# Second block's attention in a one-core network kernel: TensorE's order written out by hand, scores and transposes of a head in one stretch each

## The chip, the core and the metric

The kernel runs on one core of one Trainium2 chip. The metric is device time in microseconds (us) from start to end of one execution, as the median of several runs; lower is better. Engines are named as in the profile: PE is TensorE's matmul, PEld its weight load, DVE is VectorE, ACT is ScalarE, SP issues the DMAs.

## What is computed

The reference chains two transformer blocks on 512 tokens of width 1024. The change concerns the attention at the start of the second one, the "even" mixer: 8 heads of windowed attention (two key/value heads, distances up to 128, a slope on the distance and a learned sink) and 8 heads of neighbourhood attention (8 by 16 neighbours, learned bias), all with a root-mean-square norm per head on queries and keys:

```python
def _even_mixer(x, norm_g, w_in, qn_a, kn_a, sink_a, qn_b, kn_b, rpb_b, w_out):
    h = _rmsnorm(x, norm_g)
    qa, ka, va, qb, kb, vb = _split(h @ w_in, EVEN_SPLITS)
    qa = _rmsnorm(qa.reshape(B, S, A_KV_HEADS, A_GROUP, HEAD_DIM), qn_a)
    ka = _rmsnorm(ka.reshape(B, S, A_KV_HEADS, HEAD_DIM), kn_a)
    oa = _window_gqa(qa, ka, va, sink_a)
    qb = _rmsnorm(qb.reshape(B, S, B_HEADS, HEAD_DIM), qn_b)
    kb = _rmsnorm(kb.reshape(B, S, B_HEADS, HEAD_DIM), kn_b)
    ob = _neighbourhood_attn(qb, kb, vb, rpb_b)
    return jnp.concatenate([oa, ob], axis=-1) @ w_out
```

Its result is added to the residual `x`; a wide MLP (`mlp(0)`) follows.

## The kernel before

Everything is kept feature by token: a tile is 128 features by 512 tokens. Every fp32 product is made of three fp32r products of a high and a low half (`mm3`, L272 to L274), so every operand is first split: ACT casts the high half (`split` L286, `weight` L315) and DVE subtracts to get the low half (L287, L316). Eight PSUM banks are handed out by tag (`ps`): acc 3, sc 2, pt 2, o 1.

The stage `even` runs four kinds of step, each a generator:

- g (`begin`): one projection of 24 products of 512 columns into an acc bank, scaled by DVE (L1311), squared by ACT (L1313). f (`finish`): for a query or key tile, the column total on PE into a pt bank (L419, `total`), then the reciprocal root (`rsqrt`, ACT L295, L296, DVE L297 to L299), the gain (L1317) and the split; for a value tile, four transposes into a pt bank (L1338).
- A, B (`window`) and C, D (`neighbours`): four heads each, three steps a head, all in `softmax`. Scores: four query blocks of 128, with 256, 384, 384 and 256 keys, each in its own sc bank, three products each; DVE adds the bias and takes the maximum (L488), ACT exponentiates (L495). Then DVE multiplies by the reciprocal sum (L502), PE transposes ten 128 by 128 pieces into four pt banks (L510) and each bank is split into `Ph` and `Pl`. Then the product with the values, twelve products into the o bank, copied out by ACT (L520, or L1343 for the neighbourhood heads) to `y`.
- o (`result`): splits of the finished `y` tiles and first parts of the output projection `w_out_e`.

`EVEN_ORDER` (L69) is the order in which the program asks for these steps. It sets priorities only: a scheduler then places every instruction on its engine by its own estimate, so on PE products of projections, scores, transposes and values are mixed one by one. Each engine then runs its list strictly in order.

After the last head, `rest` finishes the output projection; `residual` (L593) adds it to `X`, and `mlp` prepares its operands from `X` two tiles at a time (`seven_x` L1472 to L1474 and splits, `seven_w` L1486 to L1488 for the weights) for the first group of MLP products (`seven_mm`).

Of the kernel before, what the change touches and what calls it, by code (L numbers as in the profile page):

```python
# [25 lines left out]
T = 512  # L26
D = 1024
# [38 lines left out]
CROSS_ORDER = "q00q01211023312233"  # L66


EVEN_ORDER = "gggfgggffgAfBgffAgfCABCDgBgADBCDAgffffBCDfBgCggADBAfgfDAfDfCCgBACfDABCBgABfCDADoBCoDCoDo"  # L69

ODD_ORDER = (
    "apggpgppapagagpaaappgpagapapaapaaapaapgapagapaaapaagappgaapaaagpagapagagpagaapaoaaagpaggpagaappa"
# [166 lines left out]
class Kernel:  # L239
# [232 lines left out]
    def softmax(self, q, k, V, e, qblk, kblk, bias, sink, y, evac):  # L472

        nc = self.nc
        qo, ko = _offsets(qblk), _offsets(kblk)
        pr = slice(64 * e, 64 * e + 64)
        P = self.tl(self.pa, [128, 1280], F32, "P", self.n_p)  # L480
        st = self.tl(self.pt, [128, 20], F32, "st", 6)
        mx, nm, sm, rs, es = (st[:, 4 * i:4 * i + 4] for i in range(5))
        for i, (c0, w) in enumerate(qblk):
            ps = self.ps("sc")
            qs = slice(128 * i, 128 * i + 128)
            self.mm3(ps[:, :w], (q[0][pr, qs], q[1][pr, qs]),
                     (k[0][pr, c0:c0 + w], k[1][pr, c0:c0 + w]), True, True)
            nc.vector.tensor_tensor_reduce(P[:, qo[i]:qo[i] + w], ps[:, :w], bias(i), 1.0,  # L488
                                           -3e38 if sink is None else sink, ALU.add, ALU.max, mx[:, i:i + 1])
        nc.vector.tensor_scalar(nm, mx, -1.0, None, op0=ALU.mult)  # L490
        if sink is not None:
            nc.scalar.activation(es, nm, AF.Exp, bias=sink)
        for i, (c0, w) in enumerate(qblk):
            b = P[:, qo[i]:qo[i] + w]
            nc.scalar.activation(b, b, AF.Exp, bias=nm[:, i:i + 1], accum_out=sm[:, i:i + 1])  # L495
        yield
        if sink is not None:
            nc.vector.tensor_tensor(sm, sm, es, op=ALU.add)
        nc.vector.reciprocal(rs, sm)
        for i, (c0, w) in enumerate(qblk):  # L500
            b = P[:, qo[i]:qo[i] + w]
            nc.vector.tensor_scalar(b, b, rs[:, i:i + 1], None, op0=ALU.mult)  # L502
        Ph = self.tl(self.pa, [128, 1280], F32R, "Ph", 2)
        Pl = self.tl(self.pa, [128, 1280], F32R, "Pl", 2)
        for j, (t0, w) in enumerate(kblk):
            pt = self.ps("pt")
            for c in range(0, w, 128):
                i = (t0 + c) // 128
                at = qo[i] + 128 * j - qblk[i][0]
                nc.tensor.transpose(pt[:, c:c + 128], P[:, at:at + 128], self.ident)  # L510
            sl = slice(ko[j], ko[j] + w)
            self.split(Ph[:, sl], Pl[:, sl], pt[:, :w])
        yield
        o = self.ps("o")
        first = True
        for j, (t0, w) in sorted(enumerate(kblk), key=lambda z: -z[1][1]):
            sl = slice(ko[j], ko[j] + w)
            self.mm3(o[:64, t0:t0 + w], V(j), (Ph[:, sl], Pl[:, sl]), first, True)
            first = False
        evac(y[pr], o[:64])  # L520
        yield

# [767 lines left out]
    def even(self):  # L1290
        nc, A = self.nc, self.A
        with self.tc.tile_pool(name="even", bufs=1) as pa:
# [1 line left out]
            xs, r, first = self.nxt()  # L1294
            rel = pa.tile([128, 384], F32, name="rel")
            nc.scalar.dma_start(rel, A["c_rel"])
            gq = pa.tile([128, 2], F32, name="gq")
            for i, n in enumerate(("q_norm_a_2", "q_norm_b_2")):
                nc.vector.tensor_scalar(gq[:, i:i + 1], self.vec(n), 0.125, None, op0=ALU.mult)
            ys = [self.tl(pa, [128, T], F32, "y", 8) for _ in range(8)]  # L1300
            self.n_p = 3

# [4 lines left out]
            def qk(name, m, gain, perm=False):  # L1307
# [4 lines left out]
                q = self.s()  # L1312
                nc.scalar.activation(q, t, AF.Square)  # L1313
                yield
                rs = self.s()
                self.rsqrt(rs, self.total(q, mat=self.hsum), 64, RMS_EPS, tmp=q)
                nc.vector.scalar_tensor_tensor(q, t, gain, rs, op0=ALU.mult, op1=ALU.mult)  # L1317
                h, l = (self.tl(pa, [128, T], F32R, "qk", 10) for _ in range(2))
                if perm:
# [26 lines left out]

            jobs, env = [], {}
            put = lambda key, gen, *args: jobs.append((key, gen(*args)))
            put("k", qk, "w_e_a", 0, self.vec("k_norm_a_2"))
            put("v", value, "w_e_a", 1)  # L1350
            put(("q", 0), qk, "w_e_a", 2, gq[:, 0:1])
            put(("q", 1), qk, "w_e_a", 3, gq[:, 0:1])
            for a in range(4):
                put(("nq", a), qk, "w_e_b", 3 * a, gq[:, 1:2], True)
                put(("nk", a), qk, "w_e_b", 3 * a + 1, self.vec("k_norm_b_2"), True)
                put(("nv", a), value, "w_e_b", 3 * a + 2, True)
                if a < 2:
                    put(("q", a + 2), qk, "w_e_a", a + 4, gq[:, 0:1])

            def begin():  # L1360
                for _, gen in jobs:
# [9 lines left out]
            def window(e):  # L1371
                for a in range(4):
                    b = self.tl(pa, [128, 384], F32, "gb", 2)
                    with self.tc.issue_after(env["normed"]):
                        nc.vector.tensor_scalar(b, rel, -(2.0 ** -(a + 4 * e + 1)), None, op0=ALU.mult)
                    bias = lambda i: b[:, 128 * (i == 0):128 * (i == 0) + BAND_Q[i][1]]
                    yield from self.softmax(env["q", a], env["k"], self.vat(env["v"], e), e, BAND_Q, BAND_K, bias,
                                            self.vec("sink_a_2", a + 4 * e), ys[a], nc.scalar.copy)

            def neighbours(e):  # L1380
                for a in range(4):
                    b = self.tl(pa, [128, 896], F32, "nb", 2)
                    nc.sync.dma_start(b, A["na_bias"][2 * a + e])
                    bias = lambda i: b[:, (0, 256, 256, 640)[i]:(0, 256, 256, 640)[i] + BAND_Q[i][1]]
                    yield from self.softmax(env["nq", a], env["nk", a], self.vat(env["nv", a], e), e, BAND_Q, BAND_K,
                                            bias, None, ys[4 + a], unperm)

            yh, yl = [None] * NK, [None] * NK
            begun = []
            early = [0, 4, 1, 5, 2, 6]  # L1390

            def split_y(ks):
                for k in ks:
                    yh[k], yl[k] = self.xtile(), self.xtile()
                    self.split(yh[k], yl[k], ys[k])

            def out(m, w, ps, ks, start, stop):
                for k in ks:
                    self.mm3(ps, (w[0][k], w[1][k]), (yh[k], yl[k]), start and k == ks[0], stop and k == ks[-1])

            def result():
                split_y(early)
                yield
                for m in range(3):
                    begun.append((self.weight("w_out_e", m, 128), self.ps()))
                    out(m, *begun[m], early, True, False)
                    yield

            run = {"g": begin(), "f": finish(), "A": window(0), "B": window(1), "C": neighbours(0),
                   "D": neighbours(1), "o": result()}  # L1410
            for c in EVEN_ORDER:
                next(run[c])
            for gen in run.values():
                assert next(gen, None) is None
            split_y([3, 7])

            def rest(m):
                if m < 3:
                    out(m, *begun[m], [3, 7], False, True)
                    return begun[m][1]  # L1420
                return self.gemm("w_out_e", m, (yh, yl))

# [330 lines left out]
```

## Time and profile before

| what | value |
|---|---|
| median of 3 runs | 2172.0 us (2170.09 to 2173.36) |
| profiled execution | 2170.15 us |
| its span, first to last instruction | 2168.4 us |
| busy share of the span: PE, DVE, ACT | 98%, 72%, 53% |
| chain that ended last: PE, DVE, ACT | 89%, 6%, 2% |
| first PE instruction that the change moves | 824.8 us |
| last value product of the attention | 1013.5 us |
| first product of the MLP's first group | 1039.2 us |

A PE row's duration contains pipeline time, so neighbouring products overlap in the table; what a product occupies is the distance from its start to the next start. "PE busy" therefore stays near 100% even where starts lie far apart. In a window's row the numbers are us of busy time, in brackets the count of instructions.

### The profile page before, as it was taken

What the parts mean: (1) busy time and instruction counts of PE and PEld (TensorE: products, weight loads), DVE (VectorE), ACT (ScalarE), POOL (GpSimd) and SP (SyncE); (2) the same over time, 40 slices, a digit from 0 to 9 for tenths busy, and PEclk for the clock granted to TensorE, in tenths of its full rate; (3) what the DMA queues carried; (4) which work ended last, traced back from release to release, by engine and by line L of the source; (5) the groups of instructions that cost most, each with busy time, mean ns of one, the idle gap of its engine ahead of it and who ended that gap; (6) DMA issues with size and microseconds to landing.
All of it is one profiled execution on the core that took longest, in us unless ns stands there. A gap on an engine that the chain in (4) does not pass through costs nothing.

```text
span 2168.4 us, 31653 instructions
## 1 busy us (share of the span) xinstructions
PE 2134.2 (98%) x11942; PEld 1804.8 (83%) x11942; DVE 1564.8 (72%) x2863; ACT 1150.8 (53%) x2100; POOL 6.0 (0%) x22
## 2 busy tenths in 40 slices
PE   8999999899999999999999999999999999999999
PEld 7877788788888897777889889888888888898997
DVE  8867858787774268887978576756776579875864
ACT  6555656665553256667645344555555456453542
POOL 0000000000000000000000000000000000000000
PEclk9999999999999999999999999999999999999999
DMA  5211241133233322211333231322222233322321
GB/s 174 70 64 64 78 142 59 49 102 102 93 98 90 91 79 85 75 65 54 128 106 101 94 106 51 112 81 78 69 71 86 68 107 117 108 98 98 106 70 68
DMA packets 94760, 192.66 MB, mean 89 GB/s; under 512 B 10512, under 2 KB 12176, under 8 KB 94608
## 3 DMA queue, kind: packets, MB, share of 16 engines
q1 hardware_dynamic: 93744, 189.01, 26.8%
q8 instruction: 93, 1.52, 0.3%
q10 hardware_dynamic: 864, 1.64, 0.2%
q14 instruction: 59, 0.48, 0.1%
HBM read 188.52 MB, written 2.10 MB: 88 GB/s over the span
## 4 chain that ended last, share of the span: by engine, by line
PE 89%; DVE 6%; ACT 2%; DMA 1%; issue 1%; SPq 0%; DVEq 0%; ACTq 0%
PE acc L272 20%; PE acc L273 20%; PE acc L274 19%; PE sc L272 6%; PE sc L274 5%; PE sc L273 5%; PE pt L274 2%; PE pt L272 2%; PE pt L273 2%; PE o L272 2%; PE o L273 2%; PE o L274 2%; PE pt L510 1%; PE sc L903 1%; PE pt L419 1%; DVE wl L316 1%
## 5 line engine op out<-in xcount | busy, mean ns | idle before, releaser
L315 ACT CAST wh<-wf 128x512 fp32r<-128x512 f32 (+1 forms) x548 | 333.9, 616 | 532.9 <-PE acc L273 429.8
L316 DVE TENSOR_TENSOR wl<-wf,wh 128x512 fp32r<-128x512 f32 (+1 forms) x548 | 369.2, 682 | 181.2 <-ACT wh L315 168.1
L272 PE MATMUL acc<-x,wh 128*128 128x512 f32 (+1 forms) x1104 | 425.2, 388 | 6.4 <-ACT x L280 5.4
L273 PE MATMUL acc<-x,wh 128*128 128x512 f32 (+1 forms) x1104 | 423.9, 385 | 0.2
L274 PE MATMUL acc<-x,wl 128*128 128x512 f32 (+1 forms) x1104 | 423.8, 385 | 0.0
L272 PEld LDWEIGHTS acc<-x,wh 128*128 128x128 f32 x1104 | 207.8, 189 | 53.0 <-ACT x L280 6.2
L273 PEld LDWEIGHTS acc<-x,wh 128*128 128x128 f32 x1104 | 208.2, 189 | 44.8 <-issue 2.9
L274 PEld LDWEIGHTS acc<-x,wl 128*128 128x128 f32 x1104 | 208.1, 189 | 43.8 <-issue 2.2
L286 ACT CAST Wh<-F 128x1792 fp32r<-128x1792 f32 x64 | 108.2, 1693 | 100.4 <-PE pt L273 66.9
L287 DVE TENSOR_TENSOR Wl<-F,Wh 128x1792 fp32r<-128x1792 f32 x64 | 129.2, 2020 | 30.9 <-ACT Wh L286 30.2
L274 PE MATMUL acc<-y,wl 128*128 128x512 f32 x288 | 113.7, 395 | 0.0
L273 PE MATMUL acc<-y,wh 128*128 128x512 f32 x288 | 113.6, 395 | 0.0
L272 PE MATMUL acc<-y,wh 128*128 128x512 f32 x288 | 113.3, 393 | 0.0
L272 PE MATMUL acc<-wh,x 128*128 128x256 f32 (+1 forms) x352 | 98.9, 281 | 0.3 <-DVE v L281 0.3
L274 PE MATMUL acc<-wh,x 128*128 128x256 f32 (+1 forms) x352 | 98.8, 281 | 0.0
L273 PE MATMUL acc<-wl,x 128*128 128x256 f32 (+1 forms) x352 | 98.8, 281 | 0.0
L274 PE MATMUL sc<-x,wl 128*128 128x512 f32 (+1 forms) x264 | 96.2, 366 | 1.1 <-DVE wl L316 1.1
L273 PE MATMUL sc<-x,wh 128*128 128x512 f32 (+1 forms) x264 | 96.0, 366 | 0.9 <-DVE x L281 0.7
L272 PE MATMUL sc<-x,wh 128*128 128x512 f32 (+1 forms) x264 | 95.0, 366 | 1.5 <-ACT x L280 1.2
L272 PE MATMUL acc<-h,wh 128*128 128x512 f32 (+1 forms) x220 | 74.1, 337 | 0.0
L274 PE MATMUL acc<-h,wl 128*128 128x512 f32 (+1 forms) x220 | 74.1, 337 | 0.0
L273 PE MATMUL acc<-h,wh 128*128 128x512 f32 (+1 forms) x220 | 74.1, 337 | 0.0
(510 smaller groups left out, 5119.9 us busy)
## 6 DMA issues: line engine op xcount, KB each, us to landing
F<-in_w_mlp_in_dram SPq DMA_DIRECT2D x64, 512.0 KB, 3.2
wf<-in_w_mlp_out_dram SPq DMA_DIRECT2D x128, 256.0 KB, 2.8
wf<-in_w_ffn_in_dram SPq DMA_DIRECT2D x88, 256.0 KB, 2.7
wf<-in_w_o_fm_dram SPq DMA_DIRECT2D x64, 256.0 KB, 2.7
wf<-in_w_in_fm_dram SPq DMA_DIRECT2D x44, 256.0 KB, 2.8
wf<-in_w_ffn_out_dram SPq DMA_DIRECT2D x40, 256.0 KB, 2.7
wf<-in_w_o_v_dram SPq DMA_DIRECT2D x32, 256.0 KB, 3.1
wf<-in_w_out_o_dram SPq DMA_DIRECT2D x32, 256.0 KB, 2.8
```

Of the source, the lines that this page charges most:

```text
L272: mm(ps, lhsT=lh, rhs=rh, start=start, stop=False, skip_group_check=True)
L273: mm(ps, lhsT=lh, rhs=rl, start=False, stop=False, skip_group_check=True)
L274: self.last_mm = mm(ps, lhsT=ll, rhs=rh, start=False, stop=stop, skip_group_check=True).ins
L286: nc.scalar.copy(hi, src)
L287: nc.vector.tensor_tensor(lo, src, self.f(hi), op=ALU.subtract)
L315: nc.scalar.copy(h[:, :n], wf[:, :n])
L316: nc.vector.tensor_tensor(l[:, :n], wf[:, :n], self.f(h[:, :n]), op=ALU.subtract)
L419: self.last_total = self.nc.tensor.matmul(ps[:, :n], lhsT=self.ones if mat is None else mat, rhs=acc[:, :n], start=True, stop=True).ins
L510: nc.tensor.transpose(pt[:, c:c + 128], P[:, at:at + 128], self.ident)
L903: mm = lambda out, pr, ss, ts: nc.tensor.matmul(out, lhsT=kq[0][pr, ss], rhs=kq[1][pr, ts], start=True, stop=True, skip_group_check=True)
```

## The change

Only `even` changes. `band_head` replaces `softmax` for these 16 heads: scores go to three banks (two blocks of 256 keys share one; the third bank is an acc bank for the first twelve heads, an sc bank for the last four), the ten transposes to three banks (the third is acc, then pt). Two of the four normalisations of a head move from DVE to ACT (`AF.Identity`, L568 of after). In `qk` one of the three DVE steps of the reciprocal root becomes an ACT square. The output projection is begun for five of its eight tiles before the end of the attention, in place of three. And the loop over `EVEN_ORDER` stands in a `manual_schedule` for PE: there the instructions keep the program's order. The letters now are g, f, o as before and S (scores of the next head), T (its transposes), V (its value product); heads follow `EVEN_HEADS`.

```diff
-EVEN_ORDER = "gggfgggffgAfBgffAgfCABCDgBgADBCDAgffffBCDfBgCggADBAfgfDAfDfCCgBACfDABCBgABfCDADoBCoDCoDo"
+EVEN_ORDER = (
+    "gggggg" "fff" "g" "f" "S" "TSgV" "TffSgV" "TfSgV" "TfSgV" "TfSgV" "TfSgV" "TfSgV" "TfSgV" "TfSgV" "TfSgV"
+    "TffSgV" "TfSoV" "TfSoV" "TSoV" "TSVo" "ToVo")
+EVEN_HEADS = "ABABCDABCDABCDCD"
...
+    def band_head(self, q, k, V, e, bias, sink, y, evac, third):
...
+        at = (0, 512, 896, 256)
+        banks = ((0, 3), (1,), (2,))
+        order = (0, 3, 1, 2)
...
+        for tag, tiles in zip(("sc", "sc", third[0]), banks):
+            ps, c, got = self.ps(tag), 0, []
+            for i in tiles:
+                k0, w = BAND_Q[i]
+                qs = slice(128 * i, 128 * i + 128)
+                self.mm3(ps[:, c:c + w], (q[0][pr, qs], q[1][pr, qs]), (k[0][pr, k0:k0 + w], k[1][pr, k0:k0 + w]),
+                         c == 0, True)
+                got.append((i, ps[:, c:c + w]))
+                c += w
+            for i, p in got:
+                red = nc.vector.tensor_tensor_reduce(part(i), p, bias(i), 1.0, -3e38 if sink is None else sink,
+                                                     ALU.add, ALU.max, mx[:, i:i + 1])
...
+        for i in order:
+            nc.scalar.activation(part(i), part(i), AF.Exp, bias=nm[:, i:i + 1], accum_out=sm[:, i:i + 1])
+        yield
...
+        for i in order:
+            if i in banks[0]:
+                nc.vector.tensor_scalar(part(i), part(i), rs[:, i:i + 1], None, op0=ALU.mult)
+            else:
+                nc.scalar.activation(part(i), part(i), AF.Identity, scale=rs[:, i:i + 1])
...
+        for tag, tiles in zip(("pt", "pt", third[1]), banks):
+            pt, c = self.ps(tag), 0
+            for j in tiles:
+                t0, w = BAND_K[j]
+                for i in range(t0 // 128, (t0 + w) // 128):
+                    b = at[i] + 128 * j - BAND_Q[i][0]
+                    nc.tensor.transpose(pt[:, c:c + 128], P[:, b:b + 128], self.ident)
+                    c += 128
+            sl = slice(at[tiles[0]], at[tiles[0]] + c)
+            self.split(Ph[:, sl], Pl[:, sl], pt[:, :c])
+        yield
...
-                rs = self.s()
-                self.rsqrt(rs, self.total(q, mat=self.hsum), 64, RMS_EPS, tmp=q)
+                rs, v = self.s(), self.total(q, mat=self.hsum)
+                nc.scalar.activation(rs, v, AF.Ln, scale=1.0 / 64, bias=self.eps_col[:, 0:1])
+                nc.scalar.activation(rs, rs, AF.Exp, scale=-0.5)
+                nc.scalar.activation(q, rs, AF.Square, scale=math.sqrt(0.5 / 64))
+                nc.vector.scalar_tensor_tensor(q, v, 64 * RMS_EPS, q, op0=ALU.add, op1=ALU.mult)
+                nc.vector.scalar_tensor_tensor(rs, q, -1.5, rs, op0=ALU.add, op1=ALU.mult)
...
             def result():
-                split_y(early)
-                yield
-                for m in range(3):
-                    begun.append((self.weight("w_out_e", m, 128), self.ps()))
-                    out(m, *begun[m], early, True, False)
+                first = [0, 4, 1, 5, 2]
+                split_y(first)
+                for m, tag in enumerate(("acc", "acc", "acc", "sc", "sc")):
+                    begun.append((self.weight("w_out_e", m, 128), self.ps(tag)))
+                    if m == 1:
+                        split_y([3])
+                        out(0, [3])
+                    if m < 4:
+                        out(m, first + [3] * (m > 0), True)
+                    else:
+                        out(m, first[:4], True)
                     yield
+                out(4, [2, 3])
+                yield
...
+            third = lambda: ("acc", "acc") if len(started) < 12 else ("sc", "pt")
...
-            for c in EVEN_ORDER:
-                next(run[c])
+            with self.tc.manual_schedule(engines={mybir.EngineType.PE}):
+                for c in EVEN_ORDER:
+                    next(run[c])
```

How the change moves instructions shows at three places. In the lists the names are those of the tiles (cm holds the identity and the matrix of the totals), and the last field is the size.

First place: PE, from the scores of the first head (the sc and first acc tiles) to its transposes (P is the head's row of probabilities). Before, the last scores and what follows them:

```order
L274 MATMUL acc_8399<-x_7765,wl_8390 128x512
L272 MATMUL acc_8399<-x_7767,wh_8389 128x512
L272 MATMUL sc_8328<-qk_8163,qk_8269 128x384
L273 MATMUL sc_8328<-qk_8164,qk_8269 128x384
L274 MATMUL sc_8328<-qk_8163,qk_8270 128x384
L272 MATMUL sc_8333<-qk_8163,qk_8269 128x256
L273 MATMUL sc_8333<-qk_8164,qk_8269 128x256
L274 MATMUL sc_8333<-qk_8163,qk_8270 128x256
L273 MATMUL acc_8399<-x_7768,wh_8389 128x512
```

After:

```order
L277 MATMUL acc_8349<-qk_8253,qk_8273 128x384
L278 MATMUL acc_8349<-qk_8254,qk_8273 128x384
L279 MATMUL acc_8349<-qk_8253,qk_8274 128x384
L577 MATMUL pt_8368<-cm,P_8333 128x128 x4
L577 MATMUL pt_8375<-cm,P_8333 128x128 x3
L577 MATMUL acc_8381<-cm,P_8333 128x128 x3
L277 MATMUL sc_8391<-qk_8253,qk_8273 128x256
```

Before, 55 rows (projections, the second head's scores, two totals) stand between this head's last scores and its first transposes; after, none.

Second place: PE at the turn from the first head's values to the second head's transposes; Ph, Pl and v are the operands of the value product, s the squared query tile of a total, 'waits' names the engine whose signal is awaited. Before, at such a turn further on:

```order
L274 MATMUL o_8561<-Ph_8460,v_1569_8148 64x256
L510 MATMUL pt_8583<-cm,P_8359 128x128 x2
L510 MATMUL pt_8588<-cm,P_8359 128x128 x3
L272 MATMUL sc_8638<-qk_8450,qk_8437 128x256
L273 MATMUL sc_8638<-qk_8451,qk_8437 128x256
L274 MATMUL sc_8638<-qk_8450,qk_8438 128x256
```

After:

```order
L279 MATMUL o_8457<-Ph_8366,v_1569_8152 64x384
L577 MATMUL pt_8479<-cm,P_8389 128x128 [waits DVE_49,PE_49]
L577 MATMUL pt_8479<-cm,P_8389 128x128 [waits Activation_49] x2
L577 MATMUL pt_8479<-cm,P_8389 128x128 [waits DVE_49]
L577 MATMUL pt_8486<-cm,P_8389 128x128 [waits PE_49]
L577 MATMUL pt_8486<-cm,P_8389 128x128 x2
L577 MATMUL acc_8492<-cm,P_8389 128x128 [waits PE_49]
L577 MATMUL acc_8492<-cm,P_8389 128x128 x2
L424 MATMUL pt_8499<-s_8201,cm 128x512 [waits DVE_49]
L424 MATMUL pt_8512<-s_8242,cm 128x512 [waits DVE_49]
L277 MATMUL sc_8528<-qk_8253,qk_8327 128x256
```

After, the totals of f, which need a pt bank, stand right behind the transposes that have just filled both.

Third place: ACT at the same turn, where the copy of the first head's values stands ahead of the casts that empty the second head's banks. After:

```order
L587 COPY y_8138<-o_8457 64x512
L291 CAST Ph_8477<-pt_8479 128x512
L291 CAST Ph_8477<-pt_8486 128x384
L291 CAST Ph_8477<-acc_8492 128x384
L1385 ACTIVATE s_8498<-pt_8499,eps 128x512
```

Before, such a turn reads so, with banks of 256 and 384 columns:

```order
L520 COPY y_8136<-o_8704 64x512
L315 CAST wh_9180<-wf_9178 128x512
L315 CAST wh_9186<-wf_9184 128x512
L286 CAST Ph_8794<-pt_8796 128x256
L286 CAST Ph_8794<-pt_8801 128x384
```

The copy and the casts are the same work; after, the first bank holds 512 columns.

## Rows read from the trace of the kernel before

**Rows 1.** The page, part 1: busy us (share of the span), instructions

```profile
PE 2134.2 (98%) x11942; PEld 1804.8 (83%) x11942; DVE 1564.8 (72%) x2863; ACT 1150.8 (53%) x2100; POOL 6.0 (0%) x22
```

**Rows 2.** Windows: stretch, length, busy us (count) of each engine, granted clock, DMA

```profile
950.00:960.00 10.00, 9.75 (x46) 6.48 (x44) 8.38 (x23) 6.56 (x14) 0.00 (x0) 1.00 0.34 111
...
1020.00:1030.00 10.00, 10.00 (x45) 8.08 (x44) 10.00 (x19) 8.77 (x15) 0.00 (x0) 1.00 0.62 210
```

**Rows 3.** Waits of PE, 800 to 1060 us: total us, times, longest

```profile
PE acc L272 <- ACT x L280: 1.4, 1, 1.4
PE sc L272 <- ACT qk L286: 0.6, 2, 0.4
```

**Rows 4.** Timeline of PE: start, us, line, tiles, shapes, count; projections, values, scores

```profile
650.64 0.39 PE L273 MATMUL acc<-x,wh 128*128 128x512 f32 x1
650.87 0.39 PE L274 MATMUL acc<-x,wl 128*128 128x512 f32 x1
...
864.38 0.28 PE L274 MATMUL o<-Ph,v 128*64 128x256 f32 x1
864.59 0.44 PE L272 MATMUL sc<-qk,qk 64*128 64x384 f32 x1
864.87 0.33 PE L273 MATMUL sc<-qk,qk 64*128 64x384 f32 x1
865.04 0.33 PE L274 MATMUL sc<-qk,qk 64*128 64x384 f32 x1
...
867.51 0.34 PE L274 MATMUL sc<-qk,qk 64*128 64x384 f32 x1
867.78 0.50 PE L274 MATMUL acc<-x,wl 128*128 128x512 f32 x1
868.12 0.39 PE L272 MATMUL acc<-x,wh 128*128 128x512 f32 x1
```

**Rows 5.** Chain that ended last, 820 to 1060 us: start, us, what

```profile
866.24 0.55 PE pt L510 x5
...
941.33 2.19 ACT P L495 x8
```

**Rows 6.** Timeline of all engines: the last value products and what follows them

```profile
1011.81 0.34 PE L272 MATMUL o<-Ph,v 128*64 128x384 f32 x1
...
1013.54 0.28 PE L274 MATMUL o<-Ph,v 128*64 128x256 f32 x1
...
1013.86 1.07 ACT L1343 COPY y<-o 64x512 f32<-64x512 f32 x1 [1.68 <-PE o L274]
```

**Rows 7.** Timeline: split of a PSUM bank of 512 columns

```profile
1001.94 0.59 ACT L286 CAST v<-pt 128x512 fp32r<-128x512 f32 x1 [1.29 <-PE pt L1338]
...
1002.56 0.69 DVE L287 TENSOR_TENSOR v<-pt,v 128x512 fp32r<-128x512 f32 x1 [0.36 <-ACT v L286]
```

**Rows 8.** Groups by line and form, 800 to 1060 us: busy us, mean ns, idle before

```profile
L502 DVE TENSOR_SCALAR P<-P,st 128x256 f32<-128x256 f32 x32 | 10.9, 344 | 0.1
...
L488 DVE CUSTOM_DVE_ANT_0 P<-sc,gb,vecs 128x384 f32<-128x384 f32 x16 | 9.8, 613 | 1.3 <-PE sc L274 1.2
...
L297 DVE SCALAR_TENSOR_TENSOR s<-s 128x512 f32<-128x512 f32 x13 | 8.8, 687 | 3.0 <-ACT s L296 2.9
...
L1343 ACT COPY y<-o 64x512 f32<-64x512 f32 x8 | 8.7, 1084 | 3.2 <-PE o L274 3.1
...
L488 DVE CUSTOM_DVE_ANT_0 P<-sc,gb,vecs 128x256 f32<-128x256 f32 x16 | 7.6, 476 | 2.1 <-PE sc L274 2.1
...
L520 ACT COPY y<-o 64x512 f32<-64x512 f32 x8 | 4.6, 575 | 3.3 <-PE o L274 3.2
```

**Rows 9.** Timeline of DVE and PE at the end of the MLP's first group

```profile
1051.08 2.49 DVE L316 TENSOR_TENSOR wl<-wf,wh 128x512 fp32r<-128x512 f32 x4
...
1058.29 1.35 DVE L287 TENSOR_TENSOR y<-F,y 128x512 fp32r<-128x512 f32 x3
```

**Rows 10.** Windows with the granted clock (columns as in group 2), elsewhere in the kernel

```profile
253.00:254.00 1.00, 1.00 (x2) 0.43 (x2) 0.75 (x2) 1.00 (x5) 0.00 (x0) 0.50 0.93 360
```

## What will it do to the time? The prediction

> **What bounds the kernel now.** I read the page's busy shares first: PE 98%, DVE 72%, ACT 53% [rows 1], so PE is the engine to shorten. The shares are means, so next come the windows over the stage: inside the attention PE is busy 9.75 of 10 us with DVE at 8.38, and behind the attention DVE is full, 10.00 of 10 us, beside a full PE [rows 2]. Third, who waits: in 800 to 1060 us PE shows seven waits, 3.7 us in all; the largest, 1.4, lies before the first instruction that the change moves, and those behind it are of the size of the second row, 1.5 us together [rows 3]. So almost nothing is to be won by removing waits: the scheduler keeps PE fed. What is left is the time that the products themselves take, and for that starts have to be read, not durations: two dense projections start 0.23 us apart [rows 4]. Everything in the stage hangs on PE's list until the last value product at 1013.54 us [rows 6]; from there DVE's list leads (the residual, the MLP's operands), full until 1058.29 + 1.35 = 1059.64 us [rows 9], where the MLP's first group ends.
>
> **Grouping the scores.** Scores contract over 64 rows, everything else over 128, and a change between the two costs. Entering: from the start of the value product at 864.38 to the third score at 865.04 are 0.66 us; the three products in it occupy 0.12 (half of 0.23), 0.17 and 0.17 by themselves, so 0.20 is lost. Leaving: from the score at 867.51 to the projection at 868.12 are 0.61 us against 0.17 + 0.23: 0.21 lost [rows 4]. A visit among other work thus costs 0.4 us. I counted visits in the order lists: 50 before, 17 after. 33 x 0.4 = **13 us gained** on PE. [...] The rows show the loss, and the measured 0.4 stands.
>
> **Grouping the transposes.** Five in one run take 0.55 us, 0.11 each [rows 5], whatever their number; the count stays 160. 0.
>
> **Moves between engines.** Two 384-column normalisations a head and one step a query or key tile leave DVE for ACT. Neither engine leads ahead of 1013.5 us, and both have idle time there [rows 2]: 0, unless their lists stand in an order that PE waits for, which comes now.
>
> **The output projection begun earlier.** Between the last value product and the first MLP product the list holds 110 products before, 55 after: 55 x 0.23 = 12.7 us of PE work move ahead of the last value product. With 13 us gained and 1.5 us of old waits gone, that product would come at 1013.5 + 12.7 - 13 - 1.5 = 1011.7 us, if PE waited for nothing new.
>
> **New waits.** Now PE keeps the program's order, and whatever waits holds all behind it. Four kinds can be seen in the lists.
>
> (a) First head: its transposes stand directly behind its scores. From the first bank on (0.9 us into 2.0 us of scores) DVE's list reads two reductions of 256 (0.48 and a short read, 0.1, each), three steps of a reciprocal root (0.69 each) and two reductions of 384 (0.61): 4.5 us, done 3.4 us behind the scores. Then four exponentials, 2.19 us [rows 5], and two normalisations of 0.34 [rows 8]; small steps some 0.3. That is **6.5 us**; without the three root steps in between, 4.5.
>
> (b) Totals behind transposes. Twelve of the sixteen heads have f between T and S; its total (or value transposes) needs a pt bank, and both were just filled. The bank comes free so: values' last product, 0.32 us until ACT's copy starts [rows 6], the copy (0.58 for windows, 1.08 for neighbourhoods [rows 8]), the cast and the subtraction of 512 columns (1001.94 to 1003.25: 1.31 [rows 7]): 2.2 or 2.7 us. PE fills 1.2 of it with transposes. Ahead of these totals stand eight window copies and four of neighbourhoods: 8 x 1.0 + 4 x 1.5 = **14 us**. If the copy came early and cast and subtraction overlapped, 8; with other work ahead on either engine, 18. Behind each waiting total are queued the next scores, a projection, the values: the head's whole period.
>
> (c) Last four heads: their third score bank is the first sc bank again, free after two reductions (0.8 us late), their third transpose bank the first pt bank again, free 2.7 us behind the values while seven transposes take 0.9 (1.9 late). 4 x 2.7 less what the last head fills with products of the output projection (2.7): **8 us**, 4 to 11.
>
> (d) DVE's list: in four heads the reciprocal that T needs stands behind the scaling of a projection that ends late, as in the third head: scaling 0.69, two weight splits 0.62 each [rows 9], a query split 0.69, a bias 0.4 and the normalisations 0.69 make 3.7 us behind the projection, and the value product covers 1.75 (1011.81 to 1013.54 [rows 6]). One of 2, three of about 1: 5; since PE late elsewhere gives them time, I take **4**, 0 to 7.
>
> Sum 6.5 + 14 + 8 + 4 = 32.5 us (16.5 to 43). Last value product: 1011.7 + 32.5 = 1044 us, 30.7 later.
>
> **What is late next.** Behind it DVE leads. Before it takes 1059.64 - 1013.54 = 46.1 us to the end of its operands. After, five weight splits of 0.62 fewer stand there (3.1), one weight preparation less (0.7), and the first residual need not wait for as many products (some 2 us): **6 us shorter**. At least 3.1; if PE's 12.7 us led there, 12.7. The MLP then ends 30.7 - 6 = 24.7 us later, and nothing behind it is changed or has slack (PE is full to the end). Against the profiled execution 2170.15 + 24.7 = 2194.9; that execution lay 1.9 us under the median 2172.0, so against the median **2197 us**.
>
> [...]
>
> **Rivals.**
> 1. The waits overlap: a wait in (b) gives DVE and ACT the time that (c) and (d) ask for, and (b) is at its lower end: 12 to 20 us of waits. 1011.7 + 16 - 1013.5 - 6 = 8, so about 2180 us. For it: DVE and ACT have 16% and 34% idle in the stage [rows 2]. Against: (a) and (b) are waits for results that take their time on idle engines too. The point from which the sign turns: waits of 7.8 us.
> 2. It is faster. ACT and DVE come ahead of PE by the moves between engines, the banks are emptied early, (a) shrinks to its 4.5, (b) to (d) vanish, and DVE's tail shrinks by the full 12.7: 1011.7 + 4.5 - 1013.5 - 12.7 = -10, so 2162; with the tail at 6, 2169. For it: the 13 us of visits are certain, and DVE is unloaded. Against: the copy of the last values cannot start before they exist, and the total waits behind it.
> 3. Clock falls: waits as forecast and the half clock in part of the stage. [...] For it: a wait in nearly every head. Against: each of some 1 us, between dense stretches.
> 4. The change doesn't group: excluded by the lists; but for four foreign products in the last head each head's twelve scores stand together.
>
> **How the numbers follow.** A measurement here tells 0.2%, 4.3 us, from no change: 2167.7 to 2176.3. Forecast (waits 20 to 43, 2184 to 2208): 0.62. Rival 1: 0.20, a quarter of it under 2176.3. Rival 2: 0.09, nearly all under 2167.7. Rival 3: 0.09. Slower 0.62 + 0.15 + 0.09 = 0.86, less 0.03 for a lean on errors common to all waits: 0.83; same 0.05 + 0.03 = 0.08; faster 0.09. The range leaves out rival 2, the nearest part of rival 1 and most of rival 3: 2174 to 2210.
>
> **What would show it.** Right: a PE wait of 5 to 7 us in front of the first head's transposes, named after DVE or ACT; some twelve waits of 1 to 1.6 us in front of L424 or L1411 for DVE's `Pl`; waits of L577 for `Pl` in the last four heads; the last value product near 1044 us; PE no longer full behind it while DVE is. Starts of scores 0.12 and 0.17 apart, 17 visits, show the 13 us. Wrong: PE dense from 825 us on, or a last value product before 1020 us, would fell (b) and (c); a clock of 0.5 within the stage would bring rival 3.

## The result: slower, and by more than forecast

| what | before | after |
|---|---|---|
| median | 2172.7 us (4 runs, 2170.1 to 2177.7) | 2230.5 us (4 runs, 2226.3 to 2234.9) |
| ratio, 95% interval | | 1.027 (1.0255 to 1.0285) |
| profiled execution, its span | 2170.15, 2168.4 us | 2234.0, 2232.3 us |
| mean granted clock of the span | 0.997 | 0.98 |
| last value product starts | 1013.54 us | 1079.37 us |

The change costs 58 us; 25 were forecast, with 2210 as the upper end of the range. Busy times of the page of after, part 1 (before: [rows 1]):

```profile
PE 2160.7 (97%) x11942; PEld 1829.4 (82%) x11942; DVE 1550.5 (69%) x2804; ACT 1174.7 (53%) x2129; POOL 6.0 (0%) x22
```

The shares hardly move: PE still reads 97%. The windows over the stage tell more (stretch, length, busy us and count of each engine, granted clock, DMA share, GB/s; before in [rows 2]):

```profile
840.00:860.00 20.00, 12.85 (x55) 9.83 (x54) 14.21 (x32) 11.53 (x25) 0.00 (x0) 0.78 0.08 27
860.00:880.00 20.00, 19.22 (x84) 14.72 (x83) 11.51 (x32) 11.48 (x26) 0.00 (x0) 0.88 0.10 27
880.00:900.00 20.00, 15.94 (x62) 12.38 (x61) 12.29 (x32) 12.18 (x30) 0.00 (x0) 0.74 0.08 27
900.00:920.00 20.00, 18.30 (x97) 13.97 (x95) 12.71 (x28) 13.15 (x29) 0.00 (x0) 1.00 0.24 76
...
940.00:960.00 20.00, 17.44 (x82) 13.89 (x81) 11.16 (x29) 12.20 (x29) 0.00 (x0) 0.83 0.12 40
...
1040.00:1060.00 20.00, 16.38 (x79) 12.90 (x78) 8.04 (x21) 9.50 (x21) 0.00 (x0) 0.82 0.08 27
1060.00:1080.00 20.00, 20.00 (x82) 15.38 (x81) 5.29 (x17) 6.58 (x16) 0.00 (x0) 0.76 0.04 13
```

Before, the whole stage in one window:

```profile
820.00:1014.00 194.00, 192.28 (x961) 141.82 (x960) 166.12 (x433) 130.60 (x311) 0.00 (x0) 1.00 0.18 59
```

Two things are new. PE is idle for up to 7 of 20 us. And the clock, 1.00 throughout this stage before, has means of 0.74 to 0.91 in seven of the thirteen windows from 820 to 1080. The row of 1060 shows why busy time misleads: PE is full there, with 82 products in 20 us; before, the stage's windows of that length hold 85 to 113.

PE's waits from 820 to 1080 us (us in total, times, longest; before in [rows 3]):

```profile
PE pt L577 <- DVE P L566: 13.2, 6, 6.7
PE pt L424 <- DVE Pl L292: 7.9, 8, 1.5
PE pt L577 <- DVE Pl L292: 4.3, 3, 1.7
PE pt L577 <- ACT P L568: 3.7, 7, 1.1
PE pt L424 <- DVE v L292: 1.9, 1, 1.9
PE pt L1411 <- DVE Pl L292: 1.5, 2, 0.7
PE sc L277 <- DVE st L550: 1.4, 3, 0.7
```

The longest is that of the first head's transposes. Timeline of DVE and PE ahead of it (start, us, engine, line, tiles, shapes; in brackets the idle time before it and what ended it):

```profile
848.53 0.68 DVE L1388 SCALAR_TENSOR_TENSOR s<-pt,s 128x512 f32<-128x512 f32 x1
...
849.67 0.69 DVE L1389 SCALAR_TENSOR_TENSOR s<-s,s 128x512 f32<-128x512 f32 x1
...
850.81 0.75 DVE L1390 SCALAR_TENSOR_TENSOR s<-s,gain,s 128x512 f32<-128x512 f32 x1
...
854.62 0.16 DVE L562 TENSOR_TENSOR st<-st 128x4 f32<-128x4 f32 x1 [1.69 <-ACT P L559]
...
855.03 0.62 DVE L566 TENSOR_SCALAR P<-P,st 128x256 f32<-128x256 f32 x2
...
855.44 2.15 PE L577 MATMUL pt<-cm,P 128*128 128x128 f32 x7 [6.70 <-DVE P L566]
```

It is the mechanism of term (a), 6.7 us against 6.5: the three root steps stand among the reductions, then come four exponentials and the first normalisation.

A total that waits behind the transposes, term (b), a neighbourhood head (timeline):

```profile
929.24 0.93 PE L577 MATMUL pt<-cm,P 128*128 128x128 f32 x7
...
929.75 1.04 ACT L1416 COPY y<-o 64x512 f32<-64x512 f32 x1
...
930.61 0.98 ACT L291 CAST Ph<-pt 128x512 fp32r<-128x512 f32 x2
931.25 1.16 DVE L292 TENSOR_TENSOR Pl<-pt,Ph 128x512 fp32r<-128x512 f32 x2 [0.68 <-ACT Ph L291]
...
932.00 1.12 PE L424 MATMUL pt<-s,cm 128*128 128x512 f32 x2 [1.51 <-DVE Pl L292]
```

Copy, cast, subtraction, total: the predicted order, and 1.51 us where 1.5 was predicted.

To compare kernels I split the stage, from the first product behind the four totals at 818 us (L419 before, L424 after) to the last value product, into three parts: waits (the idle time that the trace shows on PE), half clock (half of PE's working time at a granted 0.5), and the work that is left. The half is an estimate, rounded up from 0.46 (which would make after's 23.2 us below 21.3): in after, products of 512 columns start 0.43 us apart from 862.25 to 864.39 us, at 0.5, and 0.23 apart from 865.33 to 868.10, at 1.00. A stretch at a granted 0.5 is called a fall of the clock below.

| kernel | stage | waits | half clock | work |
|---|---|---|---|---|
| before | 194.7 | 1.7 | 0.0 | 192.9 |
| after | 255.4 | 34.5 | 23.2 | 197.7 |

So of 60.8 us more, 32.8 are waits, 23.2 the clock and 4.8 work: 57 products more of the output projection ahead of the last value product (13.2 us at 0.232 each) less 8.4, which I put down to the 33 visits saved. The remaining 5.0 of the last value product's 65.8 us are not the change's: after's profiled execution has six falls ahead of 810 us, before's three, in identical code.

The other executions agree on the clock. An execution's time multiplied by its mean granted clock estimates what it would take at full clock (idle time inside a fall is then counted to the clock). That is 2188 to 2192 us in the four executions of after, and 2162 to 2168 in those of before for which the clock is on record: about 25 of the 58 us stand without the clock, the size of the forecast, and the rest is the clock.

### The profile page after: what moved, and what is told of

Read it like the earlier page. It is cut to its first block, busy times and chain, and to the rows that moved or that the text cites. A ratio compares the mean times of both kernels' runs of the same rounds, so it can differ in the third digit from the quotient of the medians.

```text
span 2232.3 us, 31637 instructions
## 1 busy us (share of the span) xinstructions
PE 2160.7 (97%) x11942; PEld 1829.4 (82%) x11942; DVE 1550.5 (69%) x2804; ACT 1174.7 (53%) x2129; POOL 6.0 (0%) x22
## 4 chain that ended last, share of the span: by engine, by line
PE 88%; DVE 6%; ACT 4%; DMA 1%; issue 1%; SPq 0%; DVEq 0%; ACTq 0%
PE acc L277 19%; PE acc L278 19%; PE acc L279 19%; PE sc L277 6%; PE sc L279 5%; PE sc L278 5%; PE pt L279 2%; PE pt L277 2%; PE pt L278 2%; PE o L277 2%; PE o L279 1%; PE o L278 1%; PE pt L424 1%; PE sc L970 1%; ACT P L559 1%
## 5 line engine op out<-in xcount | busy, mean ns | idle before, releaser
L277 PE MATMUL acc<-x,wh 128*128 128x512 f32 (+1 forms) x1088 | 421.6, 390 | 7.3 <-ACT x L285 5.4
L279 PE MATMUL acc<-x,wl 128*128 128x512 f32 (+1 forms) x1088 | 419.3, 387 | 0.0
L278 PE MATMUL acc<-x,wh 128*128 128x512 f32 (+1 forms) x1088 | 418.9, 386 | 0.2
L292 DVE TENSOR_TENSOR Wl<-F,Wh 128x1792 fp32r<-128x1792 f32 x64 | 129.1, 2020 | 33.4 <-ACT Wh L291 32.8
L279 PE MATMUL sc<-x,wl 128*128 128x512 f32 (+1 forms) x280 | 102.7, 369 | 1.1 <-DVE wl L321 1.1
L278 PE MATMUL sc<-x,wh 128*128 128x512 f32 (+1 forms) x280 | 102.7, 369 | 0.8 <-DVE x L286 0.6
L277 PE MATMUL sc<-x,wh 128*128 128x512 f32 (+1 forms) x280 | 101.9, 370 | 0.9 <-ACT x L285 0.7
```

Source lines behind the costliest of these rows:

```text
L277: mm(ps, lhsT=lh, rhs=rh, start=start, stop=False, skip_group_check=True)
L278: mm(ps, lhsT=lh, rhs=rl, start=False, stop=False, skip_group_check=True)
L279: self.last_mm = mm(ps, lhsT=ll, rhs=rh, start=False, stop=stop, skip_group_check=True).ins
L292: nc.vector.tensor_tensor(lo, src, self.f(hi), op=ALU.subtract)
```

## Experiments

All times are medians, with the ratio to the kernel before and its 95% interval. The parts of the stage are of each profiled execution.

### Are the long waits what brings the clock down?

In the changed kernel, PE gets work of no use in the two longest waits: 26 products in front of the first head's transposes, 12 in front of the third's.

```diff
         for tag, tiles in zip(("pt", "pt", third[1]), banks):
             pt, c = self.ps(tag), 0
+            for _ in range(fill[tiles[0]]):
+                nc.tensor.matmul(pt, lhsT=self.filler[:, :128], rhs=self.filler, start=True, stop=True)
```

> The changed kernel, with 26 products whose result nobody reads put in front of the first head's transposes and 12 in front of the third head's, into the bank that the transposes then overwrite. They need 6.0 and 2.8 us at 0.23 us each, and the two waits there were 6.7 and 3.1 us, so the waits become work of no use and nothing else moves. Theory (the long waits bring the clock down): the falls at 851.3 (13.7 us at half) and 888.8 (10.2 us at half) go, worth half of 23.9 us: 2230 - 12 = about 2218 us. Rival (the clock falls for what PE executes, not for its waits): both falls stay, 2230 us.

Measured: 2220.6 us, 1.0215 (1.0193 to 1.0238): 10 us less for 8.8 us of added work. Timeline of PE at the first head, then windows (this kernel has line numbers of its own):

```profile
841.23 6.19 PE L576 MATMUL pt<-x 128*128 128x512 f32 x26
848.00 0.65 PE L581 MATMUL pt<-cm,P 128*128 128x128 f32 x2 [0.58 <-DVE P L568]
```

```profile
840.00:860.00 20.00, 19.24 (x100) 15.45 (x100) 12.64 (x39) 11.97 (x33) 0.00 (x0) 1.00 0.05 15
860.00:880.00 20.00, 17.29 (x85) 12.63 (x84) 14.17 (x31) 14.35 (x30) 0.00 (x0) 1.00 0.16 53
880.00:900.00 20.00, 19.21 (x99) 15.28 (x98) 12.48 (x37) 13.27 (x34) 0.00 (x0) 1.00 0.16 50
```

The transposes start 7.0 us behind the start of the last score, as in the changed kernel, yet the three windows that read 0.78, 0.88 and 0.74 read 1.00. The waits are the cause of these falls, and the two waits cost less filled than empty (2220.6 against 2230.5 us). It is not this execution alone: the mean granted clock is 0.988 to 0.991 in all four, 0.980 to 0.984 in the four of after. The half clock of the stage fell from 23.2 to 8.2 us, more than the 12 expected: the next fall, at 946 us in after behind three waits of 0.75 to 1.06 us, did not come in this execution although the same three waits are there (0.76, 1.05, 0.75). Its length alone thus doesn't decide whether a short wait is followed by a fall.

### Is it the written order?

```diff
-            with self.tc.manual_schedule(engines={mybir.EngineType.PE}):
-                for c in EVEN_ORDER:
-                    next(run[c])
+            for c in EVEN_ORDER:
+                next(run[c])
```

> The changed kernel without the written order: the scheduler places PE's instructions again, all other parts of the change stay. In its list the scores among the heads still stand in few stretches. Theory (the order makes the waits, and the waits the falls): 32.8 us of waits and 24 us of clock go, 9 us from fewer visits stay, 13 us of projections moved ahead are partly given back behind: 2165 to 2176 us. Rival (three banks in place of four, or the moved steps on ACT and DVE, make the waits): 2195 us and more.

Measured: 2191.7 us, 1.009 (1.0074 to 1.0106), between the two: 39 us of 58 go with the written order. Waits of PE and one window:

```profile
PE sc L277 <- ACT qk L291: 3.5, 2, 2.7
...
PE pt L1411 <- DVE Pl L292: 2.0, 2, 1.0
PE pt L424 <- DVE Pl L292: 0.8, 1, 0.8
```

```profile
840.00:860.00 20.00, 16.63 (x59) 12.22 (x59) 14.64 (x41) 8.77 (x21) 0.00 (x0) 0.64 0.08 27
```

The stage reads 217.7: waits 9.1, half clock 11.6, work 197.0. The largest part of the scheduler's own loss is one wait of 2.7 us for the first query and, behind it, the longest fall of all (17.1 us, worth 8.2). Waits for a transpose bank (L424 and L1411 for `Pl`) come to 2.8 us: three banks in place of four cost little under a scheduler.

### Which waits?

First the totals. In twelve groups of the order f and S change places, as here:

```diff
-    ... "TSgV" "TffSgV" "TfSgV" "TfSgV" ...
+    ... "TSgV" "TSffgV" "TSfgV" "TSfgV" ...
```

> The changed kernel with one thing in its order moved: the totals (and value transposes) of f stand behind the next head's scores and no longer directly behind the transposes. Theory (they wait for the two transpose banks that were just filled): their waits, 12 us in the profile, go, and with them the falls of the clock that follow the value transposes' waits (10.2 us at half, worth 5): 2230 - 17 = about 2213 us. Rival (the later query or key tile then holds the scores, or DVE's work comes later and holds the next transposes): 2225 to 2235 us.

Measured: 2206.5 us, 1.0153 (1.0138 to 1.0168): 24 us less, more than expected. Waits of PE from 820 to 1080 us:

```profile
PE pt L577 <- DVE P L566: 7.4, 2, 6.7
PE sc L277 <- DVE st L550: 4.8, 3, 3.0
PE pt L577 <- DVE Pl L292: 4.4, 3, 1.7
```

L424's waits for `Pl` are gone, and with them most of those for `P`: from 893 to 990 us PE waits 0.4 us in all. The waits of the last four heads, term (c), grew instead, from 5.7 to 9.2 us. Presumably the scores, no longer queued behind a waiting total, start each softmax earlier; that was not tried by itself. Stage: 231.4, waits 20.5, half clock 16.7, work 194.3.

Then the first head, with one projection moved between its scores and its transposes:

```diff
-    "gggggg" "fff" "g" "f" "S" "TSgV" ...
+    "ggggg" "fff" "g" "f" "S" "g" "TSgV" ...
```

> The changed kernel with one projection of 24 products put between the first head's scores and its transposes, taken from the seven ahead of the scores. Theory (the wait of 6.7 us is the first head's softmax, and the long fall of the clock follows it): 5.6 us of the wait are covered, and the fall of 13.7 us at half goes, worth 6.8: 2230 - 12 = about 2218 us. Rival (DVE is late there whatever PE does): the wait comes back in front of the totals ahead or of the third head's transposes, 2225 to 2230 us.

Measured: 2223.0 us, 1.0229 (1.0209 to 1.0249), 7.5 less. The wait shrinks from 6.7 to 1.8, but other waits of the opening stay (1.9 for the fourth total, 3.1 at the third head), and falls behind them too: half clock 21.5. The fall at the first head shrinks from 13.7 us to 6.8, but one of 3.4 us stands ahead of it now. Here, taking away one wait of several beside each other saved its length and little of the falls.

### Does the earlier output projection buy anything?

The changed kernel with three tiles begun in place of five (`for m in range(3)`, and the last three `o` dropped from the order).

> The changed kernel with the output projection begun for three of its tiles in place of five (30 products, 7.0 us, go back behind the last value product; all else, the written order too, stays). In the last head two fillers go with them: its transposes then wait for its softmax some 2.8 us more, its values for the split some 1.5. Theory (behind the last value product DVE leads, so products moved ahead of it shorten nothing there): the last value product comes 7.0 - 4.3 = 2.7 us earlier, the stretch from it to the MLP's second group keeps its 58.3 us: about 2227 us. Rival (PE leads there): that stretch grows by 7 us and the time to about 2235 us.

Measured: 2228.3 us, 1.0238 (1.0221 to 1.0255). The stage takes 249.3 us, 6.2 less than in after (2.7 were expected): 30 products fewer, 1.3 us more of waits. The last value product comes at 1068.1, and the stretch from it to the MLP's second group (its 61st product with `Th`) takes 55.2 us where after takes 58.3. So 7 us of PE work put back behind the value products made that stretch shorter, not longer: with PE short of work there, waits of 2.1, 1.4, 2.2 and 0.9 us stand in after's tail, with two falls (windows of after):

```profile
1080.00:1100.00 20.00, 16.08 (x72) 12.80 (x71) 18.29 (x29) 16.56 (x24) 0.00 (x0) 0.93 0.23 79
...
1120.00:1140.00 20.00, 16.94 (x118) 16.53 (x117) 17.58 (x26) 10.38 (x10) 0.00 (x0) 0.83 0.37 119
```

DVE leads there, as forecast: its list to the end of the MLP's first group ends 39.3 us behind the last value product here, 40.6 in after, whether 30 products more stand behind that product or not. Products moved ahead of the last value product thus shorten nothing behind it. In time the runs show little of this: the profiled execution (2219.6 us, clock 0.987) lies 9 us under the other three (2228.1 to 2228.8, clock 0.982 to 0.984), and the medians differ by 2 us, less than after's executions scatter.

### Do the moves between engines cost or gain?

The kernel before with the two ACT normalisations and the ACT square alone.

> The kernel before with one part of the change: two of four normalisations of a head and one step of each reciprocal root go from DVE to ACT; order, banks and output projection stay. Theory (neither engine leads there, PE waits 3.7 us in all): 2171 to 2175 us. Rival (PE waits behind ACT, whose list grows by 1.2 us a head and whose copies release banks): 2180 us and more.

Measured: 2175.2 us, 1.0006 (0.9996 to 1.0015): no change. In the stage DVE has 153.6 us of 201 busy (before 166.1 of 194), and PE's waits are 2.7. Without a fall in either the stage reads 196.7 against 194.7, and time multiplied by mean granted clock 2168.5 against 2164.1 beside it: a cost of a few us at full clock is possible, a gain is not seen. DVE did not set the pace there. In the written order the moves were not tried by themselves, and 3.7 us of after's waits are for the two normalisations that went to ACT (L568).

### Can the grouping gain once the waits are mended?

Totals behind the scores, one total and one projection between the first head's scores and transposes, the written order only up to the twelfth head, three tiles begun:

```diff
+    "gggg" "f" "g" "ff" "g" "S" "f" "g" "TSgV" "TSffgV" "TSfgV" ... "TSffgV")
+EVEN_LAST = "TSfoVTSfoVTSoVTSVTV"
```

> The changed kernel with the order mended: the totals stand behind the next head's scores (as in the run that moved them), the first head's scores stand one projection and one total ahead of its transposes, the written order ends with the twelfth head and the scheduler places what follows, and the output projection is begun for three tiles. Theory (waits and the falls that follow them made the whole loss): new waits of 3 to 8 us remain, the falls go, 8 us of visits are gained: 2166 to 2174 us. Rival (the clock falls for the kind of work, or DVE holds PE wherever the order lets it): 2185 us and more.

> The same as the run with the mended order, but the scheduler places every instruction and the order only sets priorities. Theory (the scheduler's loss in the run without a written order lay in its first two waits, 2.7 and 1.4 us, the two falls behind them, 12 us, and the five tiles begun, some 10): 2166 to 2176 us. Rival (its loss is spread over the three banks): about 2190 us.

Measured: 2183.6 us, 1.0038 (1.0025 to 1.0051) with the order written, 2181.3 us, 1.0035 (1.0022 to 1.0047) with the same string as priorities. Both lie between the theories. In the first, one wait of 5.3 us in front of the first total is left (the tile it sums is late, since no projection stands between the four totals at the stage's start and this one), with a fall; behind 890 us the stage has less than 5 us of waits.

Next, one projection more ahead of the first total, and the scores two heads ahead of the transposes:

```diff
+    "ggggg" "f" "g" "ff" "g" "S" "f" "S" "g" "TSfV" "TSfgV" "TSfgV" ... "TSffgV")
+EVEN_LAST = "TSfoVTSfoVTSoVTVTV"
```

> The run with the mended order, with a new opening and the scores one head further ahead: two projections are computed between the first totals, the scores of two heads stand ahead of the first transposes, and from there on the scores of head n+2 follow the transposes of head n. Theory (what was left there was the wait of 5.3 us in front of the first totals, the fall of 6.8 us at half behind it, worth 3.4, and some 2 us in front of transposes): 2183.6 - 9 = 2172 to 2178 us, the scatter of a few us from falls ahead of the stage included. Rival (DVE, late in the opening, holds PE wherever the order lets it): the wait comes back in front of the first scores, 2180 us and more.

Measured: 2173.0 us, 1.0007 (0.9994 to 1.0019): the loss is gone, and nothing is gained. Stage: 200.0, waits 9.5, half clock 1.7, work 188.8. Work is 4.2 us under before's although 24 products more (5.6 us) stand in it, so the visits are worth 9.8 us here. Behind the last value product the stretch to the MLP's second group is 5.0 us shorter than before (55.5 against 60.5). The waits eat both. Two of them:

```profile
PE sc L280 <- DVE st L553: 2.3, 1, 2.3
PE pt L580 <- ACT P L571: 2.1, 3, 1.0
```

Its executions also show the price of the clock within one kernel: those with a mean granted clock of 0.996 or 0.997 took 2169.8 to 2173.2 us, those with 0.991 took 2181.0 and 2184.0.

Three tries at the last waits:

> The same with the order written to the end of the attention: for the last heads the third bank of scores and of transposes stands apart from the first two, with six products of the output projection or a total between, and twelve such products stand behind the last value product. Theory (waits alone make the loss, and the last waits of the run with the mended order, 1.8, 0.6 and 1.8 us, are covered): 9 us of visits come out as a gain, 2164 to 2172 us. Rival (short waits of the last heads come back, since each bank is asked for again within 3 us): 2175 to 2180 us.

Measured: 2178.7 us, 1.0029 (1.0016 to 1.0043). With the end written out too (the third banks of the last heads as steps of their own), waits come to 10.6 and half clock to 10.2; work is 183.4 with 18 products fewer. The rival's waits are there: 1.4 in front of a total, 0.5, 1.0 and 0.7 in front of scores, 0.5 and 0.9 in front of transposes. But of the half clock 8.5 us lie at 844 and 878 us, in the opening, which is that of the run two heads ahead: there the same waits (1.0, 0.8; 1.0, 0.9) were followed by no fall. The comparison of the two times thus says little of the ends that differ.

> The run with the scores two heads ahead, with three of its waits taken away: the third bank of the thirteenth head's scores is an acc bank as for the heads before (wait of 2.3 us and the fall of 3.4 us behind it), the first query's total stands ahead of the value transposes (waits of 1.0 and 0.8 us in front of the first scores), and the two totals between the first two heads stand behind the second head's transposes (waits of 1.0 and 0.9 us). Theory (waits alone are left): 2172.5 - 5 to 7 = 2165 to 2169 us, faster than before by 0.1 to 0.3%. Rival (DVE is 80% busy there and sets the pace, so that a wait taken away at one place comes back at the next): 2171 to 2174 us.

Measured: 2177.0 us, 1.0016 (1.0006 to 1.0027). The thirteenth head's wait and those of the second head's transposes went, the 1.0 and 0.8 in front of the first scores did not move at all, and a new one came, in front of the scores that need the tile whose total had been put later (timeline of PE):

```profile
881.30 0.38 PE L280 MATMUL sc<-qk,qk 64*128 64x256 f32 x1 [2.94 <-ACT qk L294]
882.39 0.38 PE L281 MATMUL sc<-qk,qk 64*128 64x256 f32 x1 [0.70 <-DVE qk L295]
```

Behind it the clock falls again, worth 3.4 us. The other 5.1 of the half clock of 8.5 stand at 846 us, behind the two waits in front of the first scores, which had no fall behind them in the run two heads ahead.

> The run with the scores two heads ahead with a single edit: the third bank of the thirteenth head's scores is an acc bank in place of an sc bank that two reductions still read. Theory (the wait of 2.28 us there and the fall of 3.4 us behind it, worth 1.7, go and come back nowhere): 2172.5 - 4 = 2167 to 2170 us in executions without a fall in the stage, median about 2170. Rival (the wait comes back at the next bank, as waits did in the run before): 2171 to 2174 us.

Measured: 2173.0 us, 1.0008 (0.9996 to 1.002). The wait is gone and stayed away: waits 7.8, work 189.1; its executions begin at 2167.0. But the profiled one has a fall at 876 us behind two waits of 1 us that were there, without a fall, in the run it is compared with. No version beat the kernel before.

What is left against these versions is the clock. Time multiplied by mean granted clock, as above, has a median of 2163.8 us in the run two heads ahead and 2160.6, 2160.7 and 2161.7 in the three tries, where before has 2164.7 to 2166.0 beside them: by this estimate they need 1 to 5 us less at full clock, and a granted clock of 0.992 to 0.996 in place of 0.996 to 0.997 takes it back.

## Why the prediction was wrong

**What held.** PE's list bounds the stage, and the written order makes PE wait. The sum of new waits was 32.5 us; the trace shows 34.5 in all. By terms: (a) 6.5 against 6.7. (b) 14 against 9.4 (L424 and L1411 for `Pl`): the places were right, ten waits of 0.7 to 1.5. (c) 8 against 5.7 (L577 for `Pl`, scores for `st`). (d) 4 against 10.2 (L577 for `P` behind L566, less the first head's 6.7, and behind L568). The wait of 1.9 us for the fourth total stood in no term. Errors of both signs cancelled; the run with the totals moved shows that (b) and (d) hang together, since both fell with one edit. And 3.7 of the 10.2 are waits for ACT's normalisations, which the sum had at nothing.

**The step that failed: the clock.** The forecast took a granted 1.00 through the stage. Measured: 23.2 us of the stage are half clock. Falls of the clock stood in the third rival, but with a chance of 0.09 and the argument that the waits are of some 1 us each, between dense stretches. That argument failed. The price on which that chance was set, 20 us, was the author's estimate, and no run shows it; the runs showed 23.2 us in the stage and 6.0 in the tail. The fall that begins in the first head's wait of 6.7 us is worth 4.7 us, for which the sum had no term. The fall behind the 3.1 us at the third head is worth 5.1. The other four, 13 us, follow waits of 0.7 to 1.7 us, alone or in groups, about the size that was held to be harmless. Two rows that pointed to it stood ahead of the prediction: the half clock in a microsecond with two products begun [rows 10], and a term (a) of 6.5 us. Some of the short waits are for banks, and the windows of 20 us with the falls behind them read 0.76 to 0.91; the first fall stands in a wait of 6.7 us for a softmax. That idle time is the cause, the filled waits show for the first two falls; the run with the totals moved has no fall from 893 to 990 us, where its waits are gone and after has one; for the rest it is argued from their places.

**The visits were mis-sized.** 33 visits at 0.4 us gave 13 us; the work that is left gives 8.4, and 9.8 in the run two heads ahead (20 visits), 0.25 to 0.33 a visit. The 0.4 came from one entry behind a value product and one exit to a projection in one timeline [rows 4]; the mean over all visits was not taken.

**The tail.** DVE leads behind the last value product, as said. The end of its list for the MLP's first group, in after and in the run with three tiles begun:

```profile
1118.64 1.36 DVE L292 TENSOR_TENSOR y<-F,y 128x512 fp32r<-128x512 f32 x3
```

```profile
1105.99 1.36 DVE L292 TENSOR_TENSOR y<-F,y 128x512 fp32r<-128x512 f32 x3
```

In after it took 1118.64 + 1.36 - 1079.37 = 40.6 us where 46.1 stood before: 5.5 shorter, 6 forecast. But "nothing behind it is changed or has slack" failed in the other direction: PE waited in four places for operands, 2.2 and 0.9 us for `Wh` and `Wl` the last, and lost the clock in two falls worth 6.0 us, and the MLP's second group begins only 2.2 us nearer to the last value product than before.

Together: clock 23.2, visits 4.6, waits 1.8, tail 3.8 and 0.5 for two products more make 33.9 us beyond the forecast 24.7, so 58.6. The profiled executions differ by 63.9, of which 5.0 are falls ahead of the stage. Of the 33.9, 29 are the clock: 23.2 in the stage and 6.0 in the tail, whose other parts came out 2.2 better than forecast. That the rest of the sum is right within 5 us is in part luck, since errors of both signs cancelled.

**Chances.** The sign, at 0.83, was right. The rivals stood beside each other as alternatives, and the range left out most of the third; but the falls came on top of the forecast waits (23.2 us of half clock beside 34.5 of waits in the stage), so they belonged into the forecast's own upper end: with the 29 us of the stage and the tail, 2197 + 29 = 2226.

## What to carry to other kernels

A fixed order on a full engine is worth what its waits cost, and on PE a long wait cost twice here: its length, 6.7 us at the first head, and 4.7 us for the products behind it at a granted 0.5. So price a new wait of several us with a fall, expect falls behind waits of about 1 us too (four in after, 13 us, behind waits of 0.7 to 1.7), put the consumer of a freed bank one block of other work behind the one that filled it (24 us less with the totals moved), and where a wait can't be covered, work of no use in it was cheaper than idling (10 us less for 8.8 us of it). Products moved ahead of the last value product, behind which DVE leads, shortened nothing there (DVE's list took 40.6 us behind it in after, 39.3 with 30 products more there). And where falls scatter, compare time multiplied by mean granted clock beside the time: the three tries scatter by 15, 11 and 16 us in time, and by 2 to 5 in this product.

## What was not expected of the hardware

- A kernel's executions differ in how many falls they have, in identical code: six or three ahead of 810 us, and between 2169.8 and 2184.0 us for one kernel. Where an effect of 4 us is looked for, the falls are larger than it.
- The same short waits (0.76, 1.05, 0.75 us) were followed by a fall in one kernel and not in another. What decides was not found.
- The granted clock does not come back with the first dense product: in after, the transposes start at 855.44 us, and 4 us later PE is full and the clock still at 0.5 (a window of 4 us):

```profile
860.00:864.00 4.00, 4.00 (x12) 3.08 (x11) 2.43 (x10) 1.36 (x6) 0.00 (x0) 0.50 0.00 0
```
